# Strassen's seven products for half of the columns of a gMLP's v

## The chip, the cores and the metric

The kernel runs on one core of a Trainium2 chip. The metric is the device time of one execution in microseconds, the median of several runs. Engines are named as in the profile: PE is TensorE (PEld its weight load), DVE is VectorE, ACT is ScalarE, POOL is GpSimd, SP is SyncE, whose queue issues the loads of weights.

## The reference

A trunk of two layers over 512 frames of width 1024: layer 0 has an mLSTM mixer, layer 1 a gMLP mixer; each is wrapped by two SwiGLU FFNs and ends with a gated embedding, with a layer norm after each part. The change is in the gMLP mixer alone:

```python
def gmlp_mixer(x, w_in, b_in, vn_g, vn_b, ws, bs, w_out):
    u, v = jnp.split(jax.nn.gelu(x @ w_in + b_in, approximate=False), 2, axis=-1)
    v = layer_norm(v, vn_g, vn_b).reshape(B, NB, GM_BLOCK, GM_GROUPS, GM_GDIM)
    ...
    s = jnp.einsum('gts,bnsgc->bntgc', ws_m, v) + bs.T[:, :, None]
    return (u * s.reshape(B, S, GM_WIDTH)) @ w_out
```

x is 512 x 1024, w_in 1024 x 4096, so v is 512 x 2048.

## The kernel before

All matrix products work on split numbers: each float32 operand is held as a rounded high part (`hi`) and the rest (`lo`), and each product is three matmuls, hi x hi, hi x lo and lo x hi (`mm3`, L403 to L405). The high part is a copy by ACT (L290 for weights, L408 and L981 for activations). The low part is a subtraction on DVE (L297, L303, L409, L984), or, for some weights, a negated copy by ACT (L285) into which a DMA from POOL's queue adds the source (L286).

The class `Weights` streams all weights of the program in one order, written down ahead of it (`W.order`). SP loads them into raw buffers (`wraw`, or two half-size boxes in one, `wbox`); as split buffers come free (four of the kind `main`, two `extra` in this stage), `fill` issues the copies and low parts for the next weights. Each engine executes its instructions in the order in which the program issues them, so the place of a call in the source sets what stands ahead of what in each engine's queue.

The FFNs and the gMLP's down projection already use Strassen's algorithm in Winograd's form: two-by-two blocks of each operand, seven products instead of eight, with sums of blocks made by DVE. `Weights.forms` makes the seven forms of the weights (b11, b21, T2, T1, b12, b22, b21; `t2` and `t1` are sums, L116, L117, L121, L122), and `Group` has the forms of activations and the table `TO` which says into which block of the result product r is added. The seven products share two pairs of PSUM banks: those with even r accumulate in one pair, those with odd r in the other.

In the mixer (`gmlp`), v comes first. It is made in four chunks of 512 columns (c = 0 to 3), each for four blocks of 128 tokens (t = 0 to 3): `up_tokens` does 8 x 3 matmuls into one of four PSUM banks (`dn_bank`, tile `gvps`), DVE adds the bias into `gvf` (L1694), ACT applies Gelu (L1695), DVE takes the statistics (L1696). During chunk 0 the second half of the tokens of x is still being transposed and split (`turn_x` as hooks; `xf`, `xh`, `xl`, L658 to L669), and during chunk 1 the affine part of the previous layer norm is applied to the residual `xt` (`run_affine`: a multiplication, L784, and an addition, L788, by rows held in `gb`). In chunk 1 to 2 the spatial weights are transposed, masked and summed (`spatial_weights`, `spatial_sums`). In chunk 3 each token block's statistics are put together, and DVE scales v (L1708). Then u is made (`gups`), and the spatial products (`sps`), the gating and the down projection follow.

Of the kernel before, what the change touches and what calls it, by code (L numbers as in the profile page):

```python
# [13 lines left out]
OP = mybir.AluOpType  # L14
# [32 lines left out]
UP_BY_DMA_2 = (1, 3, 5, 6)  # L47
UP_BY_DMA_MIXED = (1, 3, 4)
UP_BY_DMA_LAST = (1, 3, 6)


class Weights:
# [4 lines left out]
    def __init__(self, nc, raw_pool, split_pool):  # L57
        self.nc = nc
        self.pools, self.free = {"main": split_pool}, {"main": W_BUFS, "none": 0}
        self.raw_pools, self.raw_bufs = {"raw": raw_pool}, {"raw": RAW_BUFS}  # L60
        self.raw_free, self.raw_at, self.raw_tags = deque(range(RAW_BUFS)), {}, {}
        self.loads, self.left, self.raws = [], [], {}
        self.queues, self.held_raws = defaultdict(deque), defaultdict(deque)
        self.order, self.next_split, self.in_place, self.by_dma = [], 0, set(), set()
        self.ready, self.taken, self.held = deque(), deque(), []
        self.apart, self.pending, self.made, self.after, self.formed = False, deque(), {}, {}, set()
        self.boxes, self.rank, self.loaded_at, self.clock = [], {}, {}, 0
        self.hold, self.limit, self.ahead, self.forced, self.sums = False, None, False, False, set()

    def open(self, kind, pool, n):  # L70
# [6 lines left out]
    def open_raw(self, kind, pool, n, tag=None):  # L77

        self.raw_pools[kind], self.raw_bufs[kind] = pool, n
        if tag:  # L80
            self.raw_tags[kind] = tag

    def add_load(self, ap, uses, kind="raw"):
        self.loads.append((ap, kind))
# [15 lines left out]

        self.order.append((kind, None, hook))

    def forms(self, kind, b11, b12, b22, b21):

        vec = self.nc.vector

        def raw(b):
            return self.raws[b[0]][b[1]]  # L110

        def as_loaded(b):
            return lambda: (raw(b), (b[0],))

        def t2():
            vec.tensor_sub(raw(b12), raw(b22), raw(b12))  # L116
            vec.tensor_add(raw(b11), raw(b12), raw(b11))  # L117
# [7 lines left out]
        made = [((b11[0],), as_loaded(b11)), ((b12[0], b22[0], b21[0]), as_loaded(b21)), ((), t2),  # L125
                ((), t1), ((), as_loaded(b12)), ((), as_loaded(b22)), ((), as_loaded(b21))]
# [3 lines left out]
        self.sums.update((t2, t1))  # L130
        return [(kind, js, make) for js, make in made]

    def up_forms(self, j11, j12, j21, j22, by_dma=UP_BY_DMA):
# [55 lines left out]
    def load(self, only=None, between=None):  # L189


        for kind, queue in self.queues.items():
            held = self.held_raws[kind]
            if kind == "raw":

                for j in [j for j in held if not self.left[j]]:
                    held.remove(j)
                    self.raw_free.append(self.raw_at[j])
            elif kind == "box":

                for j in [j for j in held if not self.left[j]]:
                    held.remove(j)
                    box, q = self.raw_at[j]
                    box[2].append(q)
                if not self.comes_next("box"):
                    for box in [box for box in self.boxes if len(box[2]) == 2]:
                        self.boxes.remove(box)
                        self.raw_free.append(box[0])
# [8 lines left out]
            if room:  # L217
# [5 lines left out]
                if kind == "raw":  # L223
                    self.raw_at[j] = at = self.raw_free.popleft()
                    raw = self.raw_pools[kind].tile([P, 2048], F32, name="wraw", tag=f"wraw{at}", bufs=1)
                elif kind == "box":
                    if not any(box[2] for box in self.boxes):
                        at = self.raw_free.popleft()
                        raw = self.raw_pools["raw"].tile([P, 2, 1024], F32, name="wbox", tag=f"wraw{at}", bufs=1)
# [143 lines left out]
def hybrid_trunk(ctx: ExitStack, tc, x, p, ln_g, ln_b, ffn1_wgu, ffn1_wd, ffn2_wgu, ffn2_wd,  # L373
# [1247 lines left out]
    def gmlp():  # L1621
        with stage_pool("extra", EXTRA) as extra, stage_pool("gm_parts") as near, stage_pool("ghpool") as hpool, \
                stage_pool("forms", 2) as fpool, stage_pool("gm") as mp:
            W.open("extra", extra, EXTRA)

            vfs = [mp.tile([P, TB, n], F32, name="gvf", tag=f"gv{i}") for i, n in enumerate((512, 512, 1024))]

            def v_cols(c, n):

                i = min(c // 512, 2)  # L1630
                return vfs[i][:, :, c - 512 * i:c - 512 * i + n]

            def v_block(b):
                return v_cols(b * P, P)


            wsp = near.tile([P, GRP, 2, P], F32R, name="wsp")
            wsh, wsl = wsp[:, :, 0], wsp[:, :, 1]

            wst2 = hpool.tile([P, 2, 2, 4, P], F32, name="wst", tag="hp")  # L1640
            wsts = [wst2[:, 0, a] for a in range(2)]
            for a in range(2):
                sca.dma_start(wsts[a], gm_ws[0, 4 * a:4 * a + 4].rearrange("g t s -> t g s"))

            def spatial_weights():
                sums = act.tile([P, 2, GRP, P], F32, name="rsum", tag="gb")
# [29 lines left out]
            next_vb = load_bias(0)  # L1676
            for c in range(4):
# [7 lines left out]
                vb = next_vb  # L1685
                for t in range(TB):
                    if t:
                        run_hook()
                    if t == 1 and c < 3:
                        next_vb = load_bias(c + 1)  # L1690
                    ps = dn_bank("gvps")
                    up_tokens(t, ws, ps, hook=run_hook if t else None, release=give_back)
                    dst = v_cols(c * 512, 512)[:, t]
                    vec.tensor_add(dst, ps, vb)  # L1694
                    sca.activation(dst, dst, AF.Gelu)  # L1695
                    vec.bn_stats(st[:, t, c], dst)  # L1696
                    if (c, t) >= (0, TB - 1):
                        run_affine()
                    if c and t < 2:
                        W.refill()  # L1700
                    if c == 3:
                        mv = small.tile([P, 2], F32, name="gmv", tag="mv")
                        vec.bn_aggr(mv, st[:, t])
                        rs = small.tile([P, 2], F32, name="grs", tag="rs")
                        vec.tensor_scalar(rs[:, 0:1], mv[:, 1:2], EPS, None, op0=OP.add)
                        pool.tensor_tensor(rs[:, 1:2], rs[:, 0:1], eps_pow, op=OP.pow)
                        def scale(v, t=t, mv=mv, rs=rs):
                            vec.tensor_scalar(v[:, t], v[:, t], mv[:, 0:1], rs[:, 1:2], op0=OP.subtract, op1=OP.mult)  # L1708
                        scale(vfs[0])
                        if t < TB - 1:  # L1710
                            scale(vfs[1])
                            scale(vfs[2])
                if c == 1:
                    rsum, bsb = spatial_weights()
                    W.open_raw("ghp", hpool, 1, "hp")
                if c == 2:
                    spatial_sums(rsum)

            def gate_u(b):
                ps = up_bank("gups")  # L1720
# [65 lines left out]

            vs = deque([split_v(0), split_v(1)])
            us, ss, hs = deque(), deque(), []
            scale(vfs[1])
            scale(vfs[2])  # L1790
            for b in range(2):
                us.append(gate_u(b))

# [193 lines left out]
```

## Time and profile before

| what | value |
|---|---|
| median of 3 runs | 2171.29 us (2171.14 to 2172.44) |
| profiled execution, its own time | 2170.96 us |
| span of the profile | 2169.2 us |
| granted clock of PE, mean | 0.999 |
| PE busy | 2158.3 us (99%), 13109 matmul records |
| DVE busy | 1762.7 us (81%) |
| ACT busy | 1238.2 us (57%) |
| POOL busy | 249.6 us (12%) |
| DMA | 342.08 MB, mean 158 GB/s |
| v stage (first to last gvps matmul) | 1487.96 to 1578.75 us of the span |

A row of the profile by time has its start, its length, engine, line, operation, what it writes and reads with shapes, and in brackets how long the engine stood idle before it and what released it. Matmuls overlap, so the distance of two starts, not the length, says how fast they go.

### The profile page before, as it was taken

The page shows a single profiled execution, that of the slowest core. Times are in us where ns is not written, and L with a number is a line of the kernel's source. Part 1 is how long each engine was busy: PE and PEld are TensorE (multiplying, and loading weights), DVE is VectorE, ACT ScalarE, POOL GpSimd, SP SyncE. Part 2 cuts the span into 40 slices and gives each one's busy share as a digit, 9 for nine tenths or more (in the row PEclk, how much of TensorE's full clock was granted, in tenths as well). Part 3 has the DMA queues.
Part 4 walks back from the last instruction along what each step waited for, and adds up shares of the span by engine and source line. Part 5 has one row for each costly group of instructions (what it writes and reads, how often), then busy time and mean ns, then how long its engine had stood idle before and what let it go on. Part 6 is the DMA issues. An engine that isn't in the chain of part 4 may idle for free. (4 is left out here: it accounts for less than half of the span.)

```text
span 2169.2 us, 33214 instructions
## 1 busy us (share of the span) xinstructions
PE 2158.3 (99%) x13109; PEld 1931.1 (89%) x13109; DVE 1762.7 (81%) x2530; ACT 1238.2 (57%) x1700; POOL 249.6 (12%) x303
## 2 busy tenths in 40 slices
PE   9999999999999999999999999999999999999998
PEld 8999998888888889999988999998888888999987
DVE  6988887777767789888887988887688688888887
ACT  4766656464646456667445666655345555666542
POOL 1111101011101111111000111100001101111100
PEclk9999999999999999999999999999999999999999
DMA  7787764366847467787445787763338748877651
GB/s 217 179 195 188 172 163 124 89 151 138 156 128 156 122 163 185 192 201 169 146 136 137 182 200 184 172 159 131 128 78 151 159 127 204 192 182 180 138 174 59
DMA packets 231683, 342.08 MB, mean 158 GB/s; under 512 B 9652, under 2 KB 164404, under 8 KB 231528
## 3 DMA queue, kind: packets, MB, share of 16 engines
q0 software_dynamic: 55680, 113.44, 31.2%
q1 hardware_dynamic: 169232, 211.83, 30.2%
q10 hardware_dynamic: 6616, 14.69, 2.1%
q8 instruction: 103, 1.69, 0.3%
q14 instruction: 52, 0.43, 0.1%
HBM read 224.58 MB, written 2.11 MB: 104 GB/s over the span
## 5 line engine op out<-in xcount | busy, mean ns | idle before, releaser
L290 ACT ACTIVATE whi<-wbox 128x1024 fp32r<-128x1024 f32 x252 | 264.3, 1053 | 222.1 <-DVE wbox L145 100.6
L404 PE MATMUL ups<-xl,whi 128*128 128x256 f32 x1152 | 326.0, 283 | 0.0
L405 PE MATMUL ups<-xh,wlo 128*128 128x256 f32 x1152 | 326.0, 283 | 0.0
L403 PE MATMUL ups<-xh,whi 128*128 128x256 f32 x1152 | 325.8, 283 | 0.0
L290 ACT ACTIVATE whi<-wraw 128x1024 fp32r<-128x1024 f32 (+1 forms) x196 | 200.8, 1046 | 91.6 <-DVE wraw L122 22.6
L403 PE MATMUL gps<-whi,fhi 128*128 128x512 f32 x644 | 252.9, 393 | 0.0
L404 PE MATMUL gps<-wlo,fhi 128*128 128x512 f32 x644 | 252.3, 392 | 0.0
L405 PE MATMUL gps<-whi,flo 128*128 128x512 f32 x644 | 251.5, 391 | 0.0
L286 POOL DMA_DIRECT2D wlo<-wbox x152 | 129.1, 849 | 951.3 <-ACT wlo L285 605.0
L404 PEld LDWEIGHTS ups<-xl,whi 128*128 128x128 f32 x1152 | 220.6, 191 | 2.6
L403 PEld LDWEIGHTS ups<-xh,whi 128*128 128x128 f32 x1152 | 220.5, 191 | 2.6
L405 PEld LDWEIGHTS ups<-xh,wlo 128*128 128x128 f32 x1152 | 220.6, 192 | 0.0
L795 DVE TENSOR_TENSOR xt<-xt,gps 128x512 f32<-128x512 f32 x302 | 195.4, 681 | 28.9 <-PE gps L405 28.9
L297 DVE TENSOR_TENSOR wlo<-wraw,whi 128x1024 fp32r<-128x1024 f32 (+1 forms) x119 | 142.3, 1212 | 34.4 <-ACT whi L290 33.5
L290 ACT ACTIVATE whi<-wquarter 128x1024 fp32r<-128x1024 f32 (+1 forms) x140 | 135.3, 966 | 58.7 <-ACT wlo L285 20.4
L285 ACT ACTIVATE wlo<-wbox 128x1024 fp32r<-128x1024 f32 x152 | 158.9, 1046 | 11.4 <-DVE wbox L153 11.4
L405 PEld LDWEIGHTS gps<-whi,flo 128*128 128x128 f32 x644 | 120.9, 188 | 27.0
L403 PEld LDWEIGHTS gps<-whi,fhi 128*128 128x128 f32 x644 | 121.3, 188 | 22.0
L404 PEld LDWEIGHTS gps<-wlo,fhi 128*128 128x128 f32 x644 | 121.4, 188 | 21.3
L303 DVE TENSOR_TENSOR wlo<-wquarter,whi 128x1024 fp32r<-128x1024 f32 (+1 forms) x116 | 139.1, 1199 | 0.0
L984 DVE TENSOR_TENSOR flo<-h,fhi 128x512 fp32r<-128x512 f32 (+1 forms) x140 | 88.8, 635 | 46.1 <-ACT fhi L981 45.7
L303 DVE TENSOR_TENSOR wlo<-wbox,whi 128x1024 fp32r<-128x1024 f32 x92 | 112.1, 1218 | 0.0
(373 smaller groups left out, 5784.3 us busy)
## 6 DMA issues: line engine op xcount, KB each, us to landing
wlo<-wbox POOLq DMA_DIRECT2D x152, 512.0 KB, 5.6
wbox<-in_ffn_wgu_dram SPq DMA_DIRECT2D x144, 512.0 KB, 4.8
wquarter<-in_ffn_wd_dram SPq DMA_DIRECT2D x64, 512.0 KB, 6.7
wraw<-in_ml_w_in_dram SPq DMA_DIRECT2D x24, 1024.0 KB, 5.6
wlo<-wraw POOLq DMA_DIRECT2D x48, 512.0 KB, 6.5
wraw<-in_gm_w_in_dram SPq DMA_DIRECT2D x15, 1024.0 KB, 5.8
wraw<-in_ffn_wgu_dram SPq DMA_DIRECT2D x17, 512.0 KB, 4.7
wraw<-in_ffn_wd_dram SPq DMA_DIRECT2D x8, 1024.0 KB, 5.0
```

The costliest lines, as they stand in the source:

```text
L285: self.nc.scalar.activation(lo[:, s], src[:, s], AF.Copy, scale=-1.0)
L286: self.nc.gpsimd.dma_start(lo[:, s], src[:, s], accum_op=OP.add)
L290: self.nc.scalar.activation(hi[:, s], src[:, s], AF.Copy)
L297: self.nc.vector.tensor_sub(lo[:, s], src[:, s], hi[:, s].bitcast(F32))
L303: self.nc.vector.tensor_sub(lo, src, hi.bitcast(F32))
L403: mm(ps, st[0], mv[0], start=start, stop=False, skip_group_check=more)
L404: mm(ps, st[0], mv[1], start=False, stop=False, skip_group_check=more)
L405: mm(ps, st[1], mv[0], start=False, stop=stop, skip_group_check=more)
L795: vec.tensor_add(dst, dst, ps)
L984: vec.tensor_sub(lo, src, hi.bitcast(F32))
```

## The change

Columns 0 to 1023 of v (chunks 0 and 1) are made by seven products over halves of tokens (256), features (512) and columns (512). Each product has two weight forms (128 x 2 x 512, over half of the features of a block each) and 2 x 2 x 2 x 3 = 24 matmuls of 512 columns. The plain chunk 2 comes first, then the seven products, then the plain chunk 3.

- Weights: forms with the low part by DMA for r = 1, 3, 4, 5, 6 (`V_BY_DMA`); r = 0 and 2 on DVE. Loads are eight boxes. After the last affine step, the buffer of `gb` is lent to the loads as one more box.
- x: the turned blocks of the last 256 tokens are left in float32 in `u` and `w`; with the joined quarters (hi + lo) in `z` and `w`, DVE makes four sums: S1 (w = u + w), S3 (u = z - u), S2 (z = w - z) and S4 (w - z). They are split into high and low parts in new buffers (`x_s`, `fhi`, `flo`).
- The affine part of the previous norm is made in chunk 2, with two of its four additions as DMAs from POOL's queue.
- Each product's banks are added into `gvf` by DVE (14 adds); Gelu and statistics come with a block's last product.
- v's scaling: DVE for columns 0 to 511, an Identity activation with scale and bias on ACT for the other 1536.
- The spatial weights are loaded later, transposed in the second block of the last chunk and summed in its third.

The core of the diff (the lines of the file after):

```diff
+V_BY_DMA = (1, 3, 4, 5, 6)
...
     def gm_weights():
-        for c in range(4):
-            add_wide(win, GW + c * 512)
+        add_wide(win, GW + 2 * 512)
+        subs = []
+        for k in (0, 2):
+            loads = [W.add_load(kp(win)[:, 4 * i + k:4 * i + k + 2, GW + j * 512:GW + (j + 1) * 512], n, "box")
+                     for i, j, n in ((0, 0, 2), (0, 1, 1), (1, 1, 1), (1, 0, 2))]
+            subs.append(W.forms("", *((j, slice(None)) for j in loads), by_dma=V_BY_DMA))
+        for both in zip(*subs):
+            W.order.extend(both)
+        add_wide(win, GW + 3 * 512)
...
+            def take(c, t, dst):
+                sca.activation(dst, dst, AF.Gelu)
+                vec.bn_stats(st[:, t, c], dst)
+
+            def scales(t):
...
+                vec.tensor_scalar(vfs[0][:, t], vfs[0][:, t], mv[:, 0:1], rs[:, 1:2], op0=OP.subtract, op1=OP.mult)
+                vec.scalar_tensor_tensor(rs[:, 2:3], mv[:, 0:1], -1.0, rs[:, 1:2], op0=OP.mult, op1=OP.mult)
+
+                def rest():
+                    for c in range(1, 4):
+                        sca.activation(vfs[c][:, t], vfs[c][:, t], AF.Identity, scale=rs[:, 1:2], bias=rs[:, 2:3])
+                return rest
...
+            def second_sum():
+                vec.tensor_add(w, u, w)
+                in_place(3, w)
+
+            def other_sums():
+                vec.tensor_sub(u, z, u)
+                vec.tensor_sub(z, w, z)
+                in_forms(2, z)
+
+            def fourth_sum():
+                joined(w, 1)
+                vec.tensor_sub(w, w, z)
+
+            new_v(2)
+            vbs = [load_bias(c) for c in (2, 0, 1)]
+            plain(2, vbs[0], ((lambda: joined(z, 0),), (lambda: run_affine(2, True),),
+                              (lambda: run_affine(2), lambda: W.lend(act, "gb"), W.fill, second_sum),
+                              (other_sums,)))
+            banks = []
+            for r in range(7):
+                if r < 2:
+                    banks.append([dn_bank("gvps", True) for _ in range(2)])
+                for k in range(2):
+                    wk = W.take()
+                    f = left[r]
+                    for e, ps in enumerate(banks[r % 2]):
+                        for kb in range(2):
...
+                            mm3(ps, st_kb, [a[:, kb] for a in wk], k + kb == 0 and r in (0, 1, 3), k + kb == 2,
+                                r not in (0, 1, 3))
+                    W.release()
+                    if r == 0:
                         W.refill()
+                if r in (0, 2):
+                    new_v(r // 2)
+                if r == 0:
+                    fourth_sum()
+                elif r == 2:
+                    in_forms(4, u)
+                elif r == 3:
+                    in_place(5, w)
+                elif r == 5:
+                    load_spatial()
+                    next_vb = load_bias(3)
+                i, j = Group.TO[r]
+                for e, ps in enumerate(banks[r % 2]):
+                    dst = vfs[j][:, 2 * i + e]
+                    vec.tensor_add(dst, ps, vbs[1 + j] if r in (0, 2, 3, 6) else dst)
+                    if r >= 5:
+                        unpin(ps)
+                    if r in (1, 4, 5, 6):
+                        take(j, 2 * i + e, dst)
+            new_v(3)
...
+            rest_scales = plain(3, next_vb, ((), (weights,), (lambda: spatial_sums(sums[0]),)))
```

`plain(c, ...)` is the body of the old loop over t, with work (`more[t]`) run after block t's statistics. `in_place` and `in_forms` copy a sum's high part by ACT and subtract it by DVE.

More of the change, by code (lines that the diff above doesn't have):

```diff
@@ L130, in forms @@
         self.sums.update((t2, t1))
+        self.by_dma.update(made[r][1] for r in by_dma)
         return [(kind, js, make) for js, make in made]
@@ L1624, in gmlp, with new_v, load_spatial @@
             W.open("extra", extra, EXTRA)
[L1626 to L1631, printed above, removed]
+            vfs = {}
+            def new_v(c):
+                vfs[c] = mp.tile([P, TB, 512], F32, name="gvf", tag=f"gv{c}")
+                return vfs[c]
             def v_block(b):
-                return v_cols(b * P, P)
+                return vfs[b // 4][:, :, b % 4 * P:(b % 4 + 1) * P]
             wsp = near.tile([P, GRP, 2, P], F32R, name="wsp")
             wsh, wsl = wsp[:, :, 0], wsp[:, :, 1]
[L1640 to L1643, printed above, removed]
+            wsts = []
+            def load_spatial():
+                wst2 = hpool.tile([P, 2, 2, 4, P], F32, name="wst", tag="hp")
+                wsts.extend(wst2[:, 0, a] for a in range(2))
+                for a in range(2):
+                    sca.dma_start(wsts[a], gm_ws[0, 4 * a:4 * a + 4].rearrange("g t s -> t g s"))
             def spatial_weights():
@@ L1674, in load_bias, with plain @@
                 return vb
-            next_vb = load_bias(0)
-            for c in range(4):
+            def take(c, t, dst):
+                sca.activation(dst, dst, AF.Gelu)
+                vec.bn_stats(st[:, t, c], dst)
+            def scales(t):
+                mv = small.tile([P, 2], F32, name="gmv", tag="mv")
+                vec.bn_aggr(mv, st[:, t])
+                rs = small.tile([P, 3], F32, name="grs", tag="rs")
+                vec.tensor_scalar(rs[:, 0:1], mv[:, 1:2], EPS, None, op0=OP.add)
+                pool.tensor_tensor(rs[:, 1:2], rs[:, 0:1], eps_pow, op=OP.pow)
+                vec.tensor_scalar(vfs[0][:, t], vfs[0][:, t], mv[:, 0:1], rs[:, 1:2], op0=OP.subtract, op1=OP.mult)
[4 more added lines that the diff above has]
+                return rest
+            def plain(c, vb, more=()):
                 ws, given = [], []
@@ L1713, in gmlp @@
[L1713 to L1717, printed above, removed]
+                    take(c, t, dst)
+                    if c == 3:
+                        if t < 2:
+                            W.refill()
+                        rest = scales(t)
+                        if t < TB - 1:
+                            rest()
+                    for work in more[t] if t < len(more) else ():
+                        work()
@@ new lines, in plain @@
+                return rest
+            quarters = [[a[:, 4 * j:4 * j + 4, 256 * i:256 * i + 256] for a in (xh, xl)] for i in (0, 1) for j in (0, 1)]
+            uw = mp.tile([P, 2, 4, 256], F32, name="x_uw", tag="gv3")
+            u, w = uw[:, 0], uw[:, 1]
+            z = mp.tile([P, 2, 4, 256], F32, name="x_z", tag="gv1")[:, 0]
+            for t in range(2):
+                s = slice(t * P, (t + 1) * P)
+                xf_to[2 + t, 0], xf_to[2 + t, 1] = u[:, :, s], w[:, :, s]
+            left = {0: quarters[0], 1: quarters[1], 6: quarters[3]}
@@ new lines, in joined, with in_forms, in_place @@
+            def joined(dst, q):
+                vec.tensor_add(dst, *(a.bitcast(F32) for a in quarters[q]))
+            def in_forms(r, f):
+                parts = [[fpool.tile([P, 2, 256], F32R, name=n, tag=n) for n in ("fhi", "flo")] for _ in range(2)]
+                for k, part in enumerate(parts):
+                    split(*part, f[:, 2 * k:2 * k + 2])
+                left[r] = parts
+            def in_place(r, f):
+                both = hpool.tile([P, 2, 4, 256], F32R, name="x_s", tag="hp")
+                split(both[:, 0], both[:, 1], f)
+                left[r] = both[:, 0], both[:, 1]
@@ L1719, in gate_u, with weights @@
+            new_v(3)
+            sums = []
+            def weights():
+                sums.extend(spatial_weights())
+                W.open_raw("ghp", hpool, 1, "hp")
+            rest_scales = plain(3, next_vb, ((), (weights,), (lambda: spatial_sums(sums[0]),)))
+            rsum, bsb = sums
             def gate_u(b):
```

42 lines of the change are left out of this document (15 added, 27 removed).

## The prediction

> **What bounds the kernel now.** I read the page's busy times first, then who waits on TensorE, then the v stage by windows, then its single rows.
>
> ```profile
> PE 2158.3 (99%) x13109; PEld 1931.1 (89%) x13109; DVE 1762.7 (81%) x2530; ACT 1238.2 (57%) x1700; POOL 249.6 (12%) x303
> ...
> PE warm L1940 <- POOL ident masks.py:199: 1.4, 1, 1.4
> PE sup L902 <- DVE wlo L297: 0.4, 1, 0.4
> PE sup L902 <- ACT whi L290: 0.3, 1, 0.3
> ```
>
> TensorE waits for 2.1 us in all, and only at the program's start. So each matmul that goes is a gain, and each new wait of TensorE is a loss: there is no idle time in which either could vanish.
>
> The v stage, cut into its four column chunks (columns: stretch, length, then busy time and instructions of each engine, clock, DMA):
>
> ```profile
> 1487.96:1511.64 23.68, 23.68 (x113) 19.60 (x112) 14.70 (x22) 14.89 (x29) 0.55 (x1) 1.00 0.33 97
> 1511.64:1533.50 21.86, 21.86 (x98) 18.06 (x97) 18.84 (x20) 7.33 (x10) 0.00 (x0) 1.00 0.43 139
> 1533.50:1556.20 22.70, 22.70 (x106) 18.95 (x105) 15.15 (x19) 7.52 (x10) 0.00 (x0) 1.00 0.49 160
> 1556.20:1578.74 22.54, 22.54 (x101) 18.64 (x100) 13.75 (x25) 5.38 (x7) 1.65 (x3) 1.00 0.29 93
> sum 90.78, PE 90.78 PEld 75.25 DVE 62.44 ACT 35.13 POOL 2.20; mean PE 22.70 PEld 18.81 DVE 15.61 ACT 8.78 POOL 0.55
> ```
>
> VectorE (DVE) is busy for 62.4 of 90.8 us. That average is not the question here; the question is what stands in its queue ahead of the row that TensorE needs.
>
> The matmuls of the second chunk:
>
> ```profile
> 1511.64 0.39 PE L403 MATMUL gvps<-whi,xh 128*128 128x512 f32 x1
> 1511.87 0.39 PE L404 MATMUL gvps<-wlo,xh 128*128 128x512 f32 x1
> ...
> 1578.53 0.39 PE L405 MATMUL gvps<-whi,xl 128*128 128x512 f32 x1
> 1578.75 0.39 PE L403 MATMUL gups<-xh,whi 128*128 128x512 f32 x1
> ```
>
> They start 0.227 us apart although each is 0.39 long, so the step is the price of one, and a product of 24 costs 5.44 us.
>
> **What goes.** Two plain chunks are 192 matmuls, seven products are 7 x 24 = 168. That is 24 x 0.227 = 5.4 us off TensorE, all on the path. The moving operand stays 512 wide, so the step stays.
>
> **What comes: VectorE's queue.** Its prices, from rows of this stage and of the Strassen down projection behind it:
>
> ```profile
> 1506.16 0.69 DVE L669 TENSOR_TENSOR xl<-xf,xh 128x512 fp32r<-128x512 f32 x1 [1.37 <-ACT xh L668]
> 1507.12 2.36 DVE L297 TENSOR_TENSOR wlo<-wraw,whi 128x1024 fp32r<-128x1024 f32 x2 [0.26 <-ACT whi L290]
> 1509.40 0.68 DVE L1694 TENSOR_TENSOR gvf<-gvps,gvb 128x512 f32<-128x512 f32 x1
> 1510.78 0.70 DVE L1696 BATCH_NORM_STATS2 gst<-gvf 128x6 f32<-128x512 f32 x1 [0.70 <-ACT gvf L1695]
> ...
> 1515.39 0.70 DVE L1696 BATCH_NORM_STATS2 gst<-gvf 128x6 f32<-128x512 f32 x1 [0.70 <-ACT gvf L1695]
> 1516.00 1.21 DVE L784 TENSOR_TENSOR xt<-xt,gb 128x1024 f32<-128x1024 f32 x1
> 1517.24 1.23 DVE L788 TENSOR_TENSOR xt<-xt,gb 128x1024 f32<-128x1024 f32 x1
> 1518.38 0.68 DVE L1694 TENSOR_TENSOR gvf<-gvps,gvb 128x512 f32<-128x512 f32 x1
> ...
> 1609.51 1.23 DVE L117 TENSOR_TENSOR wraw<-wraw 128x1024 f32<-128x1024 f32 x1
> 1611.92 1.23 DVE L297 TENSOR_TENSOR wlo<-wraw,whi 128x1024 fp32r<-128x1024 f32 x1 [0.59 <-ACT whi L290]
> ```
>
> A full row (1024 wide) takes 1.24 to a next row that reads its result (1516.00 to 1517.24) and 1.14 otherwise (to 1518.38). A half row takes 0.61 (1515.39 to 1516.00). From an add of a v block over its Gelu to its statistics are 1.38 (1509.40 to 1510.78). From a sum over its rounded copy on ScalarE (ACT) to its low part are 2.41 (1609.51 to 1611.92).
>
> Product r=2 is the place. It accumulates into the PSUM banks of r=0 (`banks[r % 2]`), so it may not start before VectorE has added r=0 into v. VectorE before, at the end of the first chunk, where gvf is v, gvps its PSUM bank and wlo a weight's low part:
>
> ```order
> L1694 TENSOR_TENSOR gvf<-gvps,gvb 128x512
> L1696 BN_STATS gst<-gvf 128x6
> L297 TENSOR_TENSOR wlo<-wraw,whi 128x1024 x2
> L1694 TENSOR_TENSOR gvf<-gvps,gvb 128x512
> L1696 BN_STATS gst<-gvf 128x6
> L784 TENSOR_TENSOR xt<-xt,gb 128x1024
> L788 TENSOR_TENSOR xt<-xt,gb 128x1024
> ```
>
> VectorE now, between the affine rows of the third token block and the low parts of r=2's weights (x_uw and x_z hold sums of x, x_s and flo their low parts, wbox the weights):
>
> ```order
> L1764 TENSOR_TENSOR x_uw<-x_uw 128x1024
> L419 TENSOR_TENSOR x_s<-x_uw,x_s 128x1024
> L1728 TENSOR_TENSOR gvf<-gvps,gvb 128x512
> L1697 BN_STATS gst<-gvf 128x6
> L1768 TENSOR_TENSOR x_uw<-x_z,x_uw 128x1024
> L1769 TENSOR_TENSOR x_z<-x_uw,x_z 128x1024
> L419 TENSOR_TENSOR flo<-x_z,fhi 128x512 x2
> L123 TENSOR_TENSOR wbox<-wbox 128x1024
> ```
>
> Directly behind it, up to the two adds of r=0 (L1811):
>
> ```order
> L124 TENSOR_TENSOR wbox<-wbox 128x1024
> L307 TENSOR_TENSOR wlo<-wbox,whi 128x1024
> L123 TENSOR_TENSOR wbox<-wbox 128x1024
> L124 TENSOR_TENSOR wbox<-wbox 128x1024
> L307 TENSOR_TENSOR wlo<-wbox,whi 128x1024
> L128 TENSOR_TENSOR wbox<-wbox 128x1024
> L129 TENSOR_TENSOR wbox<-wbox 128x1024
> L128 TENSOR_TENSOR wbox<-wbox 128x1024
> L129 TENSOR_TENSOR wbox<-wbox 128x1024
> L1750 TENSOR_TENSOR x_uw<-xh,xl 128x1024
> L1774 TENSOR_TENSOR x_uw<-x_uw,x_z 128x1024
> L1811 TENSOR_TENSOR gvf<-gvps,gvb 128x512 x2
> ```
>
> What moved: the sums for r=2, for r=3 and even for r=5 (L1774) stand ahead of the adds of r=0, which are the first thing TensorE needs.
>
> The same for ScalarE, whose copies gate VectorE's low parts. Before, behind the transposed x:
>
> ```order
> L290 ACTIVATE whi<-wraw 128x1024 x2
> L1695 ACTIVATE gvf<-gvf 128x512
> L290 ACTIVATE whi<-wraw 128x1024 x2
> L1695 ACTIVATE gvf<-gvf 128x512 x2
> L290 ACTIVATE whi<-wraw 128x1024
> ```
>
> and now:
>
> ```order
> L300 ACTIVATE whi<-wbox 128x1024 x2
> L1696 ACTIVATE gvf<-gvf 128x512
> L418 ACTIVATE x_s<-x_uw 128x1024
> L300 ACTIVATE whi<-wbox 128x1024
> L295 ACTIVATE wlo<-wbox 128x1024
> L300 ACTIVATE whi<-wbox 128x1024
> L295 ACTIVATE wlo<-wbox 128x1024
> L1696 ACTIVATE gvf<-gvf 128x512
> ```
>
> The four copies of r=1's weights now wait behind the copy of a sum of x, and the fourth block's Gelu waits behind them.
>
> ScalarE's prices, and those of the low parts made by DMA:
>
> ```profile
> 1506.04 1.99 ACT L290 ACTIVATE whi<-wraw 128x1024 fp32r<-128x1024 f32 x2
> ...
> 1592.10 3.89 ACT L290 ACTIVATE whi<-wraw 128x1024 fp32r<-128x1024 f32 x4
> ...
> 1604.11 0.62 ACT L981 ACTIVATE fhi<-gvf 128x512 fp32r<-128x512 f32 x1
> ...
> 1610.83 1.06 ACT L290 ACTIVATE whi<-wraw 128x1024 fp32r<-128x1024 f32 x1 [5.58 <-DVE wraw L117]
> ...
> wlo<-wbox POOLq DMA_DIRECT2D x152, 512.0 KB, 5.6
> ```
>
> The first 23.68 us (a plain chunk with the last transposes of x) stay as they are, but for the joined quarter of x (one full row, L1750), which fits into VectorE's idle 1.4 us between two xl rows, and two multiplications by gb that move ahead of the last xl rows, beside ScalarE's copies. So VectorE reaches the low parts of r=0 at 1507.12 as before, and then, in its order:
>
> - two low parts, to the row at 1509.40; add, Gelu, statistics: 1510.78 + 0.61 = 1511.39
> - four affine rows, 2 x (1.24 + 1.14): 1516.15. (The other two additions go by DMA, on POOL's queue, ahead of r=1's low parts; they land long before.)
> - the sum S1 to its low part 2.41, and 1.14: 1519.70
> - the fourth block's add. ScalarE starts S1's copy at 1516.15 + 1.32 (1609.51 to 1610.83) = 1517.47, then 0.97, the four copies 3.89 and the Gelu 0.67: statistics at 1523.00, done 1523.61
> - S3 and S2: 1.24 + 1.22, two half copies on ScalarE (the first 0.62, with 0.08 of handing over), two half low parts 1.21: 1527.98
> - r=2's two weights, each 1.24 + 2.41 + 1.14: 1537.56
> - r=3's two weights, each 1.24 + 1.14: 1542.32
> - r=5's sum, 1.24 + 1.14: 1544.70
> - the first add of r=0, 0.68: 1545.4.
>
> Without a wait r=2 would start at 1511.64 + 2 x 5.44 = 1522.5. TensorE is therefore **22.9 us late** there. Inside this lies a smaller wait: r=1's low parts are issued only after ScalarE's copies, at about 1520.5, and land 5.6 later, so r=1 ends near 1531; r=2's wait covers it.
>
> Behind r=2 the queues are about even. r=4 needs the adds of its bank, behind S3's low parts, whose copies stand on ScalarE behind four copies for r=5 that wait for r=2's end (1545.4 + 5.4 = 1550.8): 3.9 + 1.3 + 1.3 + 0.7 gives about 1557.3, and r=3 ends at 1556.3. **1.0 us.** The lows of r=3 to r=6 are issued 4 us or more ahead of need beyond their 5.6, so they cost nothing; should a landing take longer, the next products wait. In the last chunk the sums of the spatial weights (4 matmuls) come after three token blocks and need their low parts from VectorE. From r=6's end VectorE has some 18 us of rows (two pairs of adds left over 8, two u weights 2.3, two blocks with their scaling about 6, wsp 2.2) and TensorE 17: between 0 and 2.4 us, I take the middle, rounded up, **1.5**.
>
> v's scaling now is:
>
> ```profile
> L1708 DVE TENSOR_SCALAR gvf<-gvf,gmv,grs x12: 541/546/811, 1567.3 to 1587.5; 128x512 f32<-128x512 f32 x8, 128x1024 f32<-128x1024 f32 x4
> ```
>
> Of that, 4 x (0.55 + 0.81) = 5.4 us move to ScalarE as 12 half rows of 0.62; ScalarE is busy 5.38 of 22.5 us in the fourth chunk, so it is hidden. The additions of bias and the loads are off the path.
>
> Sum: -5.4 + 22.9 + 1.0 + 1.5 = **+20.0 us**. The profiled execution took 2170.96 (span 2169.2), 0.3 below the median of 2171.29; so 2191.0.
>
> **The clock.** The first rows of TensorE in this trace are transposes after idleness:
>
> ```profile
> 1.43 3.67 PE L1940 MATMUL warm<-ident 128*128 128x128 f32 x16 [1.43 <-POOL ident masks.py:199]
> ...
> 7.10 1.25 PE L1940 MATMUL warm<-ident 128*128 128x128 f32 x10
> ```
>
> 0.229 us each against 0.125: the first 3.7 us ran at about half speed. A second such loss after the wait of r=2 would be 16 x 0.104 = 1.7 us, and the one after r=1's wait is covered. The sum would be 2192.7. I don't add it, since no pause inside the program is in this trace. [...]
>
> **Rivals.**
> - TensorE keeps pace and only the 5.4 us count: 2165.5, faster. For it: VectorE gets 16 full and 10 half rows more (26 us) and loses four low parts, two additions and the scaling (13 us), so its 62.4 busy us rise to only about 75 of 85. Against it: r=0's adds stand behind 38 us of rows that can't start before x is turned at 1506. It decides if the adds of r=0 come before 1522.5, which needs 23 us fewer. Chance 4%.
> - VectorE never waits for ScalarE: from 1507.12 stand 22 full rows and 7 half ones, 22 x 1.14 + 7 x 0.61 = 29.4, r=2 starts at 1536.5, 14 late: 2170.96 + 14 - 5.4 = 2179.6, with the later waits 2182. Against it: sum, copy and low part follow from each other. Chance 13% for 2176 to 2186.
> - The loss of clock as above, 2192.7: a chance of one in two, inside my range.
> - The later products wait as well, since DMA lows land more than 4 us later than the median 5.6, or the adds of r=5 and r=6 fall behind: 4 us for two products, 2200. Chance 10%.
> - The two cancel, within 0.2% (4.3 us, about what can be told from no change): 3%.
>
> The forecast, 2186 to 2196, holds 70%. The range of 2181 to 2199 leaves out the fast case, the lower half of the second and the upper half of the fourth rival. Faster 0.04, same 0.03, slower 0.93.
>
> **What would show it.** Right: TensorE has waits of some 2 and 6 us in r=1 and of 14 before r=2's first matmul, released by VectorE's adds L1811; 24 matmuls fewer at the same step; VectorE busy without a break but for ScalarE's copies from 1507 to 1545. Wrong: r=2 starts before 1536, or r=3 to r=6 wait long for low parts (wlo by DMA).

## The result and the profile after

The changed kernel takes 2202.2 us (median of 4 runs, 2201.0 to 2206.6) beside 2171.3 for the kernel before on the same chip: a ratio of 1.0145, 95% interval [1.0127, 1.0162], so slower by 31 us. The forecast was 2191.0, with a range that ended at 2199. The profiled execution took 2201.03, its span is 2199.2 against 2169.2, and the difference that the trace has to explain is 30.0 us.

Busy times on the page, and all waits of TensorE in the stretch from 1480 to 1640 us (columns: who waited for whom, us in total, times, longest):

```profile
PE 2159.0 (98%) x13085; PEld 1929.8 (88%) x13085; DVE 1776.5 (81%) x2546; ACT 1266.0 (58%) x1734; POOL 259.4 (12%) x315
...
PE gvps L413 <- ACT whi L300: 15.4, 2, 13.2
PE rsps L1685 <- DVE wsp L1677: 6.5, 1, 6.5
PE gvps L414 <- DMA wlo<-wbox: 5.2, 1, 5.2
PE gvps L413 <- DVE gvf L1811: 1.4, 1, 1.4
```

The 24 matmuls are gone (13109 to 13085). In their place stand 28.5 us of waits, all in the v stage, where there were none. The first line names a releaser that had long been done: ScalarE made the high part of r=2's first weight at 1530.08 (first row below), and VectorE its low part at 1531.17. What ended the 13.2 us is seen in TensorE's and VectorE's rows (timeline: start, length, engine, line):

```profile
1530.08 1.06 ACT L300 ACTIVATE whi<-wbox 128x1024 fp32r<-128x1024 f32 x1 [3.29 <-DVE wbox L124]
...
1545.14 0.77 PE L413 MATMUL gvps<-whi,fhi 128*128 128x512 f32 x1 [13.18 <-ACT whi L300]
1545.70 0.63 PE L414 MATMUL gvps<-wlo,fhi 128*128 128x512 f32 x1
1546.13 0.63 PE L415 MATMUL gvps<-whi,flo 128*128 128x512 f32 x1
...
1548.95 0.39 PE L413 MATMUL gvps<-whi,fhi 128*128 128x512 f32 x1
```

```profile
1543.16 1.23 DVE L1774 TENSOR_TENSOR x_uw<-x_uw,x_z 128x1024 f32<-128x1024 f32 x1
1544.31 1.28 DVE L1811 TENSOR_TENSOR gvf<-gvps,gvb 128x512 f32<-128x512 f32 x2
```

r=5's sum (L1774) runs, then the two adds of r=0 (L1811), and 0.83 us after the start of the first of them r=2 begins. The working put that add's end at 1545.4; r=2 began at 1545.14.

The second thing to see is the step. Behind the pause the matmuls stand 0.43 us apart and not 0.227, until 1548.95. Nine steps took 3.81 us, where nine at full speed take 2.04: 1.8 us lost. The granted clock, the number before the last two, says the same:

```profile
1545.14:1548.69 3.55, 3.55 (x9) 2.78 (x9) 1.30 (x3) 3.26 (x4) 1.36 (x2) 0.50 1.01 192
1549.00:1552.00 3.00, 3.00 (x15) 2.49 (x14) 1.41 (x3) 2.25 (x3) 0.03 (x1) 1.00 1.01 186
```

The same happens behind r=1's pause (hidden under r=2's wait) and behind the one of the spatial sums:

```profile
1592.82 0.39 PE L415 MATMUL gvps<-whi,xl 128*128 128x512 f32 x1
...
1599.69 0.77 PE L1685 MATMUL rsps<-wsp,ones_r 128*128 128x512 f32 x1 [6.49 <-DVE wsp L1677]
1600.26 0.68 PE L1686 MATMUL rsps<-wsp,ones_r 128*128 128x512 f32 x1
...
1603.56 0.39 PE L415 MATMUL gvps<-whi,xl 128*128 128x512 f32 x1
```

From these rows: r=2 starts 22.6 us after the 1522.5 at which it would start without a wait; half speed behind it 1.8; a pause of 1.6 before the last chunk's plain blocks (1575.71, the 1.4 of the table and the hand-over); the spatial sums 6.87 - 0.23 = 6.6; half speed behind them, nine steps in 3.87, 1.8; less the 5.4 of the matmuls. That is 29.0 of 30.0. The last 1.0 I did not follow; u begins 29.2 later (1607.91 where it was 1578.75), so most of it arises behind the v stage.

Why the spatial sums are late is read backwards through ScalarE and VectorE:

```profile
1571.50 1.06 ACT L300 ACTIVATE whi<-wraw 128x1024 fp32r<-128x1024 f32 x1 [2.44 <-DMA wraw<-in_gm_w_in_dram]
```

```profile
1572.60 2.36 DVE L307 TENSOR_TENSOR wlo<-wraw,whi 128x1024 fp32r<-128x1024 f32 x2 [2.81 <-ACT whi L300]
...
1592.26 0.69 DVE L1697 BATCH_NORM_STATS2 gst<-gvf 128x6 f32<-128x512 f32 x1 [2.30 <-ACT gvf L1696]
1597.61 1.29 DVE L1675 TENSOR_TENSOR wsp<-wsps,wsp 128x512 fp32r<-128x512 f32 x2 [2.83 <-ACT wsp L1674]
```

The low parts of the last chunk's second weight wait until 1572.6 for ScalarE, which waits until 1571.5 for a load. The adds and statistics of r=5, r=6 and of the plain blocks stand behind them row by row, and the spatial weights' low parts (wsp) come last. The load is late because SP's queue holds it back. SP's waits between 1549 and 1575, then what was issued on two queues, from 1552 to 1560 and in the microsecond from 1561 (last column: median us to landing):

```profile
SPq L254 <- DMA wlo<-wbox: 20.2, 2, 12.2
```

```profile
wlo<-wbox POOLq DMA_DIRECT2D x3, 512.0 KB, 8.6
```

```profile
wraw<-in_gm_w_in_dram SPq DMA_DIRECT2D x1, 1024.0 KB, 10.1
```

A low part made by DMA was issued at 1552.57; with a landing of 8.6 us instead of the 5.6 of before it is there at 1561.2. Until then it holds its box, and the load that needs the room is issued at 1561 and lands 10.1 us later (5.3 for such loads in this stretch before). From 1560 to 1580 the DMA engines are busy without a break (the number before the last is their share: 0.19 before, in the first line, and 1.01 now):

```profile
1560.00:1580.00 20.00, 20.00 (x90) 16.57 (x89) 12.43 (x23) 4.75 (x6) 1.65 (x3) 1.00 0.19 66
...
1560.00:1580.00 20.00, 18.57 (x82) 15.04 (x82) 13.10 (x16) 9.35 (x12) 0.86 (x1) 1.00 1.01 274
```

So there seem to be two chains: VectorE's queue up to r=2, and behind it the boxes, the loads and VectorE once more. The experiments test both.

### The profile page after: what moved, and what is told of

Read it like the earlier page. It is cut to its first block, busy times and chain, and to the rows that moved or that the text cites. A ratio compares the mean times of both kernels' runs of the same rounds, so it can differ in the third digit from the quotient of the medians.

```text
span 2199.2 us, 33284 instructions
## 1 busy us (share of the span) xinstructions
PE 2159.0 (98%) x13085; PEld 1929.8 (88%) x13085; DVE 1776.5 (81%) x2546; ACT 1266.0 (58%) x1734; POOL 259.4 (12%) x315
## 5 line engine op out<-in xcount | busy, mean ns | idle before, releaser
L300 ACT ACTIVATE whi<-wbox 128x1024 fp32r<-128x1024 f32 x266 | 278.7, 1053 | 230.0 <-DVE wbox L153 100.7
L296 POOL DMA_DIRECT2D wlo<-wbox x162 | 137.3, 848 | 998.2 <-ACT wlo L295 648.4
L300 ACT ACTIVATE whi<-wraw 128x1024 fp32r<-128x1024 f32 (+1 forms) x188 | 192.4, 1046 | 94.9 <-DVE wraw L129 22.6
L295 ACT ACTIVATE wlo<-wbox 128x1024 fp32r<-128x1024 f32 x162 | 169.3, 1045 | 15.5 <-DVE wbox L161 11.4
L307 DVE TENSOR_TENSOR wlo<-wraw,whi 128x1024 fp32r<-128x1024 f32 (+1 forms) x111 | 132.7, 1213 | 37.5 <-ACT whi L300 36.7
```

Source lines behind the costliest of these rows:

```text
L295: self.nc.scalar.activation(lo[:, s], src[:, s], AF.Copy, scale=-1.0)
L296: self.nc.gpsimd.dma_start(lo[:, s], src[:, s], accum_op=OP.add)
L300: self.nc.scalar.activation(hi[:, s], src[:, s], AF.Copy)
L307: self.nc.vector.tensor_sub(lo[:, s], src[:, s], hi[:, s].bitcast(F32))
```

## The experiments

Times are medians of 4 runs each (10 in e6), beside runs of the kernel before on the same chip (medians 2171.2 to 2171.8). The intervals of e1 to e5 and of e7 to e9 all overlap with that of the changed kernel, so a gain of 2 or 3 us there is believed only where the rows of the trace show it too.

### The first chain: r=0's adds

**e3_add_first**: r=0's adds ahead of the second release.

```diff
+                    if r == 0 and k:
+                        new_v(0)
+                        for e, ps in enumerate(banks[0]):
+                            vec.tensor_add(vfs[0][:, e], ps, vbs[1])
                     W.release()
...
-                for e, ps in enumerate(banks[r % 2]):
+                for e, ps in enumerate(banks[r % 2] if r else ()):
```

> The changed kernel with the two adds of r=0 issued ahead of the second release of r=0, that is ahead of the sums for the second weight of r=2, for r=3 and for r=5. Theory (r=2 waits for the adds of r=0, because of VectorE's order): r=2 starts at about 1533 instead of 1545; its second half waits for its own weight's low part to 1538; r=3 then waits for its low part by DMA, which lands at about 1547.7, 1.2 later than before, and starts slowly; r=3 ends near 1555 instead of 1557.8. So 12 us of the wait go and most of it comes back one product later: 3 us fewer, about 2199. Rival (r=2 waits for its own weights, as the profile's releaser ACT whi has it): r=2 starts at 1545 as before, 2202.

Measured 2201.7, ratio 1.014 [1.0125, 1.0155]. Waits of TensorE in the same stretch:

```profile
PE gvps L413 <- ACT whi L300: 6.7, 3, 3.5
PE rsps L1685 <- DVE wsp L1677: 6.5, 1, 6.5
...
PE gvps L413 <- DVE gvf L1797: 1.1, 1, 1.1
```

r=2 now starts at 1533.34, 11.8 us earlier, released by the moved adds (L1797): the place of the wait is shown. Yet the time stays. TensorE is held again at r=2's second half, at r=3 (1546.51) and inside r=3, and the spatial sums start at 1600.83 where they started at 1599.69. Ending the first wait alone is worth nothing: VectorE has the same rows to do, and TensorE meets them one product later.

**e5_no_affine**: the affine part of the previous norm is left out for all four token blocks, so x lacks it. That is six rows on VectorE, four of them in the queue between the second block's statistics and S1, and two additions by DMA.

```diff
-            plain(2, vbs[0], ((lambda: joined(z, 0),), (lambda: run_affine(2, True),),
-                              (lambda: run_affine(2), lambda: W.lend(act, "gb"), W.fill, second_sum),
+            plain(2, vbs[0], ((lambda: joined(z, 0),), (lambda: affine.clear(),),
+                              (lambda: W.lend(act, "gb"), W.fill, second_sum),
```

> The changed kernel without the affine part of the norm ahead of the mixer (multiplication by and addition of the rows in gb; this part of the computation is left out). VectorE loses 4.8 us of rows between the second block's statistics and the sum S1, and 2.3 ahead of them, which were hidden. Theory (the wait of r=2 is the length of VectorE's chain, row by row): r=2 starts 4.8 us earlier, at 1540.4, and all behind it too: about 2197.4. Rival (r=2 is held by r=1's low parts by DMA or by ScalarE): these come earlier by as much only in part, less than 2 us.

Measured 2196.8, ratio 1.0118 [1.0103, 1.0133]. r=2 starts 4.5 us earlier, and the end comes 5.4 earlier:

```profile
1540.62 0.77 PE L413 MATMUL gvps<-whi,fhi 128*128 128x512 f32 x1 [12.95 <-ACT whi L300]
...
1595.39 0.76 PE L1685 MATMUL rsps<-wsp,ones_r 128*128 128x512 f32 x1 [6.51 <-DVE wsp L1677]
```

Four rows of VectorE at 1.2 us each are worth nearly their own length, at r=2 and, with 4.3 us, at the spatial sums alike. No other single change that leaves the sums in their place moved them by as much. So the length of VectorE's queue sets the start of r=2. For the spatial sums the run does not part the two chains, since ScalarE gets the last chunk's load 4.3 us earlier as well (1567.21 where it was 1571.50).

### The clock

**e4_busy**: 54 matmuls ahead of r=2 into a bank that nobody reads.

```diff
+                if r == 2:
+                    busy = up_bank("busy")
+                    for n in range(54):
+                        mm(busy, xh[:, 0, 0:P], xh[:, 0], start=n == 0, stop=n == 53)
```

> The changed kernel with 54 matmuls more, of x's first tile with itself into a free PSUM bank that nobody reads, ahead of r=2's. They need 54 x 0.227 = 12.3 us and fit into the pause of 13.3 us. Theory (after the pause TensorE goes at half speed for some 3.5 us, which costs 2 us): the first matmuls of r=2 step by 0.23 instead of 0.43, 2.0 us fewer: about 2200.2. Rival (the slow matmuls wait for VectorE's or ScalarE's rows or their ports, not for the clock): they stay slow, 2202 or some tenths more.

Measured 2202.1, ratio 1.0141 [1.0126, 1.0156].

```profile
1545.79 0.47 PE L413 MATMUL gvps<-whi,fhi 128*128 128x512 f32 x1 [0.61 <-ACT whi L300]
1546.10 0.40 PE L414 MATMUL gvps<-wlo,fhi 128*128 128x512 f32 x1
1546.33 0.39 PE L415 MATMUL gvps<-whi,flo 128*128 128x512 f32 x1
...
1576.83 0.47 PE L413 MATMUL gvps<-whi,xh 128*128 128x512 f32 x1 [2.79 <-DVE gvf L1815]
1577.13 0.50 PE L414 MATMUL gvps<-wlo,xh 128*128 128x512 f32 x1
1577.43 0.63 PE L415 MATMUL gvps<-whi,xl 128*128 128x512 f32 x1
...
1600.80 0.47 PE L1685 MATMUL rsps<-wsp,ones_r 128*128 128x512 f32 x1 [4.87 <-DVE wsp L1677]
```

With TensorE kept busy r=2 shows no slow step (0.31 to the second matmul, then 0.23): the half speed is a consequence of the pause and not of r=2's operands. But the time does not fall. The pause before the plain blocks grows from 1.4 to 2.8 us, with half speed behind it there (steps of 0.43, until 1580.78), and the spatial sums start at 1600.8. That speaks for a second chain that does not ask TensorE.

### The second chain: spatial sums, scaling, loads

**e2_sums_late**: the sums of the spatial weights after the fourth token block, not the third.

```diff
-rest_scales = plain(3, next_vb, ((), (weights,), (lambda: spatial_sums(sums[0]),)))
+rest_scales = plain(3, next_vb, ((), (weights,), (), (lambda: spatial_sums(sums[0]),)))
```

> The changed kernel with one call moved: the sums of the spatial weights (4 matmuls) come after the fourth token block of the last chunk instead of after the third. Theory (the pause of 6.5 us ahead of these matmuls is a wait for VectorE's wsp rows, which come at 1600.1, and 2 us more go to slow matmuls behind it): TensorE's fourth block runs in that time and only some 1.6 us of waiting are left, so 7 us fewer: about 2195. Rival (VectorE and ScalarE are behind by that much in any case, so the wait comes back at the first spatial products): 2200 to 2203.

Measured 2198.7, ratio 1.0133 [1.0116, 1.015]. The expected gain came to one half:

```profile
PE sps L1850 <- DVE rsum L1687: 1.1, 1, 1.1
PE rsps L1685 <- DVE wsp L1677: 1.1, 1, 1.1
PE sps L1851 <- DVE gvl L419: 0.7, 1, 0.7
```

The pause of 6.5 us and its half speed are gone, but three waits of together 2.9 us come in their place, because VectorE itself is behind: its wsp rows came no earlier.

**e8_busy_late**: e2 and e4 together.

> The spatial sums after the fourth block, and 54 idle-weight matmuls that keep TensorE busy ahead of r=2, whose results nobody reads. Theory (behind r=2 VectorE and the loads set the end, not TensorE): no gain over the spatial sums alone, about 2198.7. Rival (TensorE sets it): the 2 us of half speed at r=2 are gained, 2196.7.

Measured 2198.3, ratio 1.0122 [1.0105, 1.0139]: no gain over e2 alone. r=2 ran at full step from 1545.67, and the plain blocks began at 1576.32 after a wait of 2.49. So behind r=2 it is not TensorE that sets the end.

**e1_scale_dve**: v's scaling back on VectorE.

```diff
-vec.scalar_tensor_tensor(rs[:, 2:3], mv[:, 0:1], -1.0, rs[:, 1:2], op0=OP.mult, op1=OP.mult)
...
-sca.activation(vfs[c][:, t], vfs[c][:, t], AF.Identity, scale=rs[:, 1:2], bias=rs[:, 2:3])
+vec.tensor_scalar(vfs[c][:, t], vfs[c][:, t], mv[:, 0:1], rs[:, 1:2], op0=OP.subtract, op1=OP.mult)
```

> The changed kernel with v's scaling all on VectorE again, as before the change. Theory (the twelve activations of 0.74 us on ScalarE are not hidden: three of them hold up the second block's Gelu by 1.6 us and the copies of the spatial weights by 2.2, but VectorE's own three rows of 0.55 per block stand in the same chain): the low parts of the spatial weights come some 1.2 us earlier, about 2201. Rival one (the scaling on ScalarE makes the whole wait of 6.5 us): 2196 to 2198. Rival two (it is hidden): 2202.

Measured 2201.3, ratio 1.0139 [1.0124, 1.0154]; 0.9 us, within the spread of either kernel, but the wait shows it more plainly:

```profile
PE rsps L1685 <- DVE wsp L1677: 4.6, 1, 4.6
```

It was 6.5. ScalarE's copies of the spatial weights run at 1592.40 there, and at 1597.00 in the changed kernel, where three Identity passes stand ahead of them:

```profile
1594.87 0.81 ACT L1710 ACTIVATE gvf<-gvf,grs 128x512 f32<-128x512 f32 x1 [2.65 <-DVE grs L1706]
1595.59 1.50 ACT L1710 ACTIVATE gvf<-gvf,grs 128x512 f32<-128x512 f32 x2
1597.00 1.05 ACT L1674 ACTIVATE wsp<-wsps 128x512 fp32r<-128x512 f32 x2
```

**e6_before_scale_act**: the other half of that test, the kernel before with only that part of the change, three quarters of v's scaling on ScalarE.

```diff
-                            vec.tensor_scalar(v[:, t], v[:, t], mv[:, 0:1], rs[:, 1:2], op0=OP.subtract, op1=OP.mult)
-                        scale(vfs[0])
+                            for h in range(0, v.shape[2], 512):
+                                w = v[:, t, h:h + 512]
+                                sca.activation(w, w, AF.Identity, scale=rs[:, 1:2], bias=rs[:, 2:3])
```

> The kernel before with only the last part of the change: three quarters of v scaled by ScalarE. Theory (hidden, since no other step waits for ScalarE there): TensorE waits for nothing new, 2171.3 within 0.5. Rival (the activations delay Gelu and so the end of v): 1 to 3 us more.

Measured 2172.7 against 2171.6, ratio 1.0006 [0.9996, 1.0015]: about one microsecond more, past the half that the theory allowed and at the lower end of the rival's, but not clear of the spread. A new wait of 0.5 us is in its trace:

```profile
PE gups L403 <- ACT guf L1726: 0.5, 1, 0.5
```

The scaling is a small part of the loss in both kernels.

**e7_one_load**: the last chunk loads one of its two weights and uses it twice, so its blocks of v are other numbers.

```diff
-        add_wide(win, GW + 3 * 512)
+        W.add((kp(win)[:, 0:4, GW + 3 * 512:GW + 4 * 512], half4 + half4))
```

> The changed kernel with only the first of the last chunk's two weight loads (1 MB), whose tile is used for both halves of the features (so this part computes with other weights). Theory (behind r=2 the chain that ends in the wait of 6.5 us runs through this load: its buffer comes free only when r=5's low parts are made, it lands at 1571.5, and VectorE stands 2.8 us and ScalarE 2.4 before it): VectorE's queue moves up by 2.4 and the wait shrinks by as much, about 2199.8; the loads behind it land sooner too, which may add 1 or 2 us. Rival (the chain behind r=2 is set by VectorE's and ScalarE's own rows, not by this load): 2202.

Measured 2200.3, ratio 1.0131 [1.0116, 1.0146]: 1.9 us less, near what was expected. It did not come where the theory had it: the wait of the spatial sums is 6.9 and not shorter. What is gone is the wait before the plain blocks, and the spatial sums start at 1598.45, 1.2 us earlier. The late load costs; the loads are on the path.

**e9_pairs**: both adds of a product, then both Gelus, then both statistics, instead of one block after the other.

```diff
-                    if r in (1, 4, 5, 6):
-                        take(j, 2 * i + e, dst)
+                for e in range(2 if r in (1, 4, 5, 6) else 0):
+                    sca.activation(vfs[j][:, 2 * i + e], vfs[j][:, 2 * i + e], AF.Gelu)
+                for e in range(2 if r in (1, 4, 5, 6) else 0):
+                    vec.bn_stats(st[:, 2 * i + e, j], vfs[j][:, 2 * i + e])
```

> The changed kernel with another order within each product of r = 1, 4, 5, 6: both adds, both Gelus, both statistics, where now the second add stands behind the first statistics. VectorE's idle 0.7 us before each statistics goes, 1.37 us for each pair. Theory (VectorE's queue behind the late load sets the end of the chain): the pairs of r=5 and r=6 count, about 2.7 us fewer, 2199.5; if r=4's counts too, 2198. Rival (the load or TensorE sets it): 2202.

Measured 2199.2, ratio 1.0132 [1.0117, 1.0147]: 3.0 us less, near the 2.7 expected. VectorE waits for fewer Gelus, and the sums start 2.1 us earlier:

```profile
PE rsps L1685 <- DVE wsp L1677: 3.7, 1, 3.7
```

### All of the order, and what still holds it

**c1_order** joins e1, e2, e3 and e9. It also puts r=1's adds ahead of its release, calls for r=5's sum only behind r=2, makes r=3's low parts on VectorE, and holds r=3's weights back until r=1's adds are in the queue (the limit below). The split of S1 moves behind r=0's first release, and the spatial weights are transposed in the first block of the last chunk and not in the second.

```diff
-V_BY_DMA = (1, 3, 4, 5, 6)
+V_BY_DMA = (1, 4, 5, 6)
...
+            W.limit = t1_at[0]
```

> All of VectorE's order taken in hand at once: the adds of r=0 and of r=1 go ahead of the second release, each pair together; the transfers that make r=3's weights are held back until then; r=3's low parts are made by VectorE; pairs of adds, Gelus and statistics together; v's scaling on VectorE as before; the spatial sums after the fourth block. Theory (VectorE's queue and the late loads set the end, row by row): r=2 starts near 1530 instead of 1545, r=3 ends some 8 us earlier, the last block's spatial sums no longer wait; 2189 to 2190. Rival (the last chunk's loads, which can start only when r=3's boxes are free, hold the end whatever the order is): about 2196, with the wait in r=5 and r=6.

Measured 2194.0, ratio 1.0103 [1.0088, 1.0118]: 8 us less than the changed kernel, and between the two expectations.

```profile
PE gvps L413 <- DVE gvf L1799: 5.6, 1, 5.6
PE gvps L413 <- DVE gvf L1825: 5.4, 1, 5.4
PE gvps L413 <- ACT whi L300: 3.3, 1, 3.3
PE gvps L414 <- DMA wlo<-wbox: 1.5, 1, 1.5
...
```

r=2 starts at 1530.5 as expected, and the spatial sums wait for nothing. What was not foreseen is the second line, 5.4 us before r=4 (1556.89). Nor was the clock: the slow steps behind the waits at r=2, r=3 and r=4 last until 1535.6, 1549.3 and 1562.9 and cost 2.4, 2.9 and 2.8 us, worked out as above. Together that is 8.1 us, where this order loses 22 in all.

**c2_split_first** was to take that wait away.

```diff
+                    elif r == 2 and k:
+                        new_v(1)
+                        in_forms(4, u)
                     W.release()
```

> The order of the run before with one more repair: the split of r=4's x sums is called for ahead of r=2's second release, so that ScalarE makes its high part before the sixteen passes on r=4's boxes and not behind them. Theory (the wait of 5.4 us before r=4 is ScalarE's row: high part of r=4's sum behind those passes, VectorE's low part behind that, r=2's additions behind that): the wait and the half speed behind it go, but r=3's second weight comes some 1.5 us later; 2189 to 2191. Rival (the loads of the last chunk, issued at the same 1548, hold the end): the wait moves to r=5 and r=6 and the time stays at 2193 to 2194.

Measured 2194.4, ratio 1.0103 [1.0086, 1.012]. The run decides nothing, because the edit hardly moved what it was to move. Six of ScalarE's passes on the weights of r=4 and r=5 (eight in c1; the expectation said sixteen) are called for by r=2's first release, and stay ahead of the split, which moved on ScalarE from 1554.21 to 1552.23 only; and the fourth sum's two rows came between VectorE's low parts and the adds:

```profile
1552.87 1.29 DVE L419 TENSOR_TENSOR flo<-x_uw,fhi 128x512 fp32r<-128x512 f32 x2 [4.98 <-ACT fhi L418]
1554.09 1.22 DVE L1752 TENSOR_TENSOR x_uw<-xh,xl 128x1024 f32<-128x1024 f32 x1
1555.34 1.23 DVE L1775 TENSOR_TENSOR x_uw<-x_uw,x_z 128x1024 f32<-128x1024 f32 x1
1556.60 1.29 DVE L1826 TENSOR_TENSOR gvf<-gvps,gvb 128x512 f32<-128x512 f32 x2
```

**c3_adds_first** puts the fourth sum and r=2's adds ahead of those low parts.

```diff
                     elif r == 2 and k:
+                        fourth_sum()
                         new_v(1)
+                        for e, ps in enumerate(banks[0]):
+                            vec.tensor_add(vfs[1][:, e], ps, vbs[2])
                         in_forms(4, u)
```

> The order of the two runs before, and now the fourth sum and r=2's additions go ahead of the low part of r=4's x sum on VectorE, all called for ahead of r=2's second release. The last run moved the split by only 2 us and put the fourth sum's 2.5 us between it and the additions, so r=4 began no earlier; here the additions come at about 1551 and r=4 begins near 1553.5 instead of 1557.4. Theory (TensorE's wait before r=4 is worth what it lasts): the end comes 3 to 4 us earlier, 2190 to 2191. Rival (the loads of the last chunk, still issued at 1548 and some 10 us on the way, set when the plain blocks start, near 1576): the wait is found again ahead of the plain blocks, at 3 to 4 us, and the time stays at 2193.5 to 2194.5.

Measured 2194.1, ratio 1.0101 [1.0085, 1.0118].

```profile
1552.97 0.50 PE L413 MATMUL gvps<-whi,fhi 128*128 128x512 f32 x1 [1.46 <-ACT fhi L418]
...
1555.94 0.77 PE L414 MATMUL gvps<-wlo,fhi 128*128 128x512 f32 x1 [2.46 <-DMA wlo<-wbox]
...
1576.54 0.77 PE L413 MATMUL gvps<-whi,xh 128*128 128x512 f32 x1 [2.61 <-DVE gvf L1827]
```

```profile
1572.34 1.06 ACT L300 ACTIVATE whi<-wraw 128x1024 fp32r<-128x1024 f32 x1 [5.01 <-DMA wraw<-in_gm_w_in_dram]
```

r=4 begins 4.5 us earlier than in c2, and all of it is given back: 2.5 to a low part made by DMA, 2.6 before the plain blocks. ScalarE has nothing to do for 5.0 us and waits for the last chunk's load, which lands at 1572.3 (1571.5 in the changed kernel). The rival of this run was right. Whatever the order of VectorE's queue, in the changed kernel and in c1 to c3, ScalarE gets that load between 1571.5 and 1572.7. In c1 the plain blocks start at 1576.08 without a wait: there TensorE, late from its own waits and slow steps, and the load come out even. So two limits seem to lie close together, and taking away one meets the other. None of these orders goes below 2194, 22 us above the kernel before. An order in which the boxes come free earlier was not tried.

## Why the prediction was wrong in its size

- **Removed matmuls, -5.4**: 24 fewer at the same step of 0.227. Right, except where the step was 0.43.
- **r=2 late, +22.9**: right, in cause and size. The first add was forecast to start at 1544.70 and started at 1544.31, r=2 was forecast for 1545.4 and began at 1545.14, and e3 and e5 show that the adds of r=0 and the rows ahead of them are the reason. The waits in r=1 were 2.2 and 5.2, forecast some 2 and 6.
- **The clock, "I don't add it"**: failed. It cost 1.8 behind r=2, where the text had worked out 1.7, and 1.8 once more behind the spatial sums, a pause that the forecast took as 1.5 us (one of 1.43, before the plain blocks, brought no slow step). That 1.7 came so near is luck in part, since the same loss is 1.5 to 2.9 in the other runs. The trace after has what the trace before had no row for: half speed for 3.8 us behind the pause of 13.2. But e4 and e8 also show that at r=2 this 1.8 is not what sets the end.
- **r=4's wait, +1.0**: 0. The working is also added up wrongly: 1550.8 + 3.9 + 1.3 + 1.3 + 0.7 is 1558.0 and not 1557.3, so the term would have been 1.7. The two adds that r=4 needs started at 1556.37 and took 1.28; r=2 ran slower than the working had it, r=3 ended at 1557.8 and not at 1556.3, and the adds had the time.
- **The spatial sums' wait, +1.5**: failed, and the largest error: 6.6, with 1.8 of half speed behind it. The term counted VectorE's rows from r=6's end as if they could all run at once. They could not: they wait for ScalarE (2.3 and 2.8 us in the rows shown), which has Identity passes in its queue, and they start late.
- **"The additions of bias and the loads are off the path"**: false for the loads. The load of the last chunk is issued at 1561, behind the boxes, and lands 10.1 us later (e7, c3). The pause of 1.6 before the plain blocks is from the same cause and was in no term.
- **"The lows of r=3 to r=6 … cost nothing"**: they landed in 8.6 where 5.6 was taken. No product of the changed kernel waited for them, as the text said; their boxes did, and with those the load.
- **v's scaling "is hidden"**: mostly. e1 takes 1.9 us off the wait of the spatial sums and 0.9 off the time.

So the sum failed behind the start of r=2, by 9 us in five terms (clock, r=4, plain blocks, spatial sums, and 0.3 at r=2 itself) and by the 1.0 that was not followed, and not at the place it was built on. Of the rivals the last but one (landings more slowly, the adds of r=5 and r=6 behind, 2200), given 10%, came nearest, though no product from r=3 to r=6 waited as it has it.

## What to carry to other kernels

When two products share a bank, the add that frees it has to stand in its engine's queue ahead of all work for later products; but moving it alone gains nothing if the same queue is full behind it (in e3 r=2 began 11.8 us earlier and the time went from 2202.2 to 2201.7), so count that queue to the end of the stage and not only to the first wait. A tile from which a DMA makes something was held here until that DMA landed (8.6 us; SP's queue waited 20.2 us for two such landings): put the landing, not the issue, into the due time of every load that needs the room. And a wait is priced with the slow steps behind it, 1.5 to 2.9 us each in these runs where they came (1.43 us of waiting, and 2.49 in e8, brought none); whether they show in the end depends on what else is late there (e4).

## What the runs showed of the hardware

- **The granted clock fell to one half in the pauses.** Worked out from stretches of 0.25 us, it falls to 0.50 in the changed kernel at 1521.43, 1535.09 and 1596.53, inside the waits of 5.2, 13.2 and 6.5 us, and is back at 1.00 at 1528.27, 1548.74 and 1603.36. So it was low for 6.84, 13.65 and 6.83 us. In the kernel before, with no wait of TensorE in this stage, it is 1.00 from 1500 to 1610. In c1 its mean is 0.98 from 1500 to 1530, 0.75 from 1530 to 1557 and 0.87 from 1557 to 1580.
- **Which pauses brought the slow step.** In c3 2.61 us did (0.43 from 1577.10 on), in e4 2.79 us. The 2.49 us of e8 (0.31 to the second matmul, then 0.23) and the 1.43 us of the changed kernel did not. What decides at which moment the clock falls was not shown.
- **The slow stretch differs in length.** It took 3.0 us in e7 at r=2 (1545.52 to 1548.56) and 6.1 in e7 at r=1 (1525.30 to 1531.42), which cost 1.5 and 2.9 us beside full steps.
- **Short pauses together.** In c3 waits of 1.46 and 2.46 us with one matmul between them brought the slow step (0.57 from 1555.94 on), and in e3 waits of 1.04 and 0.76 us, also with one matmul between (0.44 from 1538.64 on).
- **Landings under load.** A 512 KB low part by DMA took 5.6 us in the median over the program before, and 8.6 in the median of the three issued between 1552 and 1560, where loads ran beside them. A 1 MB load took 5.3 in the median of this stretch before (1500 to 1580), and the one issued at 1561 took 10.1, while the DMA engines were busy for 20 us without a break.
